# Hand-ordered ScalarE and VectorE queues in the mixers' main stretch, with softmax and weight parts staged a quarter chunk apart

## The chip, the cores and the metric

The kernel runs on one core of one Trainium2 chip. The metric is the device time of one execution in microseconds (us), the median of several executions.

## The reference

A two-layer encoder over 256 tokens with 1024 channels, everything in fp32. Each layer adds half a SwiGLU block, then three parallel token mixers, then half a second SwiGLU block:

```
x = x + 0.5 * swiglu(rmsnorm(x), w_ffn1_in, w_ffn1_out)
h = rmsnorm(x)
qa, ka, va, qb, kb, vb, qc, kc, vc, gate_logits = split(h @ w_in)
y_a = softmax attention, 8 heads on 2 key heads, q/k rmsnorm and axial rotary
y_b = windowed attention, 8 heads on 2 key heads, bias, a sink logit in the sum
y_c = 4 heads of (softmax1 - lambda * softmax2), bias, rmsnorm of the output
x = x + sum_n(sigmoid(gate_n) * (y_n @ w_branch_n)) @ w_out
x = x + 0.5 * swiglu(rmsnorm(x), w_ffn2_in, w_ffn2_out)
```

After the second layer a last rmsnorm gives the output.

## The kernel before

**Products in three parts.** Every fp32 operand of a big product is split in a high part (rounded to fp32r) and a low part (the rest), and `mm3` (L318) issues three matmuls for each product: high by high, high by low, low by high. The weights come in chunks of 1 MB. For each chunk SP issues a load into a `raw` tile (three buffers), ScalarE casts it to `hi` in two halves (L306) and VectorE subtracts to get `lo` (L307), each with three buffers. `weights()` (L312) hands out chunk i; before that it issues loads up to chunk i+4 and the splits up to chunk i+2, both halves one after the other.

**The mixer's main stretch.** `mixer(l)` first projects keys, queries and values of mixer A and turns the keys into `kas` (L999 to L1002, under `high_priority`). Then it walks a generator `rest()` (L925) over the other chunks in the order of `ORDER` (L39): queries of B, gates (g), keys and queries of C, and the branch products (r). A chunk `fm` (L814) is 48 matmuls on TensorE and yields four times, 0.5 credits each, so a yield is a quarter of a chunk, and a chunk counts 2.0. Its result leaves PSUM on VectorE; for a gate a Tanh on ScalarE follows at once (L847).

**The steps.** 24 softmax units (8 heads of A, 8 of B, 4 of C with two maps each) run through a plan of 32 steps. In step s, TensorE transposes the probabilities of unit s-3 (`transpose_p`, L611), makes the value product of unit s-5 (`pv`, L628), and makes the scores of unit s (`scores`, L604). For a unit of A or B these are four 128-column transposes, four matmuls and four matmuls. Round the scores lie a maximum on VectorE, two Exp on ScalarE, a reciprocal on VectorE and two scalings on ScalarE (`normalize`, L648). Round the transposes lie `pth` (ScalarE, L617) and `ptl` (VectorE, L618). Behind the value product lies `head_out` (L636): a copy on ScalarE (L638) and an add on VectorE (L639). `half()` (L101) gives the value product one of two halves of a single PSUM bank in turn. The loop at L1012 takes a step for every 1.25 credits (`PACE`), and the first as soon as 1.25 are there; it starts with 0.75, and the first yield adds 0.5. The first step is therefore issued behind the first quarter of chunk b1. The steps also issue SP's loads of the bias tiles `G` (L623). C's queries and keys are split in pieces that the list `later` hands out one by one.

**What sets the order.** TensorE follows the program. ScalarE and VectorE follow the program only inside `manual_schedule(engines=BY_HAND)`, which here stands round the start and round the last product of the kernel; everywhere else, the mixers included, a scheduler orders their instructions when the program is compiled. SP and POOL are always ordered by it.

Of the kernel before, what the change touches and what calls it, by code (L numbers as in the profile page):

```python
# [31 lines left out]
NBK = 32  # L32


PACE = 1.25
D1, D2, D3 = 3, 2, 2


# [29 lines left out]
def encoder(ctx: ExitStack, tc: tile.TileContext, a, rope, onehot, out):  # L68
# [240 lines left out]

    used = [0]  # L310

    def weights(more=True):  # L312
        i = used[0]
        used[0] += 1
        ahead(i + 5, i + 3 if more else i + 2)
        return parts[i]

    def mm3(ps, w, k, sl, xh, xl, first, last, start=None):  # L318
# [334 lines left out]
    def mixer(l):  # L653
        T = {}

        def soft_a(h):
            sc = scores(T["qa"][h // 4], (h // 2) % 2, h % 2, T["kas"], h // 4)
            sA = T["sA"]
            nb = sm.tile([P, 2], F32, name="nb")
            nc.vector.reduce_max(out=nb, in_=sc, axis=AX.X)  # L660
            nc.vector.scalar_tensor_tensor(out=nb, in0=nb, scalar=-1.0, in1=sA[:, :, h], op0=ALU.mult, op1=ALU.mult)
            e = t2("e")
            su = sm.tile([P, 2], F32, name="su")
            for qt in range(2):
                nc.scalar.activation(out=e[:, qt, :], in_=sc[:, qt, :], func=AF.Exp, bias=nb[:, qt:qt + 1], scale=sA[:, qt, h:h + 1], accum_out=su[:, qt:qt + 1])
            normalize(e, su)
            return e

        def biased(sc, G, init, su):

            nb = sm.tile([P, 2], F32, name="nb")
            e = t2("e")
            for qt in range(2):
                u0 = 128 * (1 - qt)
                nc.vector.tensor_tensor_reduce(out=e[:, qt, :], in0=sc[:, qt, :], in1=G[:, u0:u0 + S], scale=1.0, scalar=init, op0=ALU.add, op1=ALU.min, accum_out=nb[:, qt:qt + 1])
            for qt in range(2):
                nc.scalar.activation(out=e[:, qt, :], in_=e[:, qt, :], func=AF.Exp, bias=nb[:, qt:qt + 1], scale=-1.0, accum_out=su[:, qt:qt + 1])
            return e, nb

        def soft_b(h):  # L680
            sc = scores(T["qb"][h // 4], (h // 2) % 2, h % 2, T["kbs"], h // 4)
            sk = sink[:, l, h:h + 1]
            su = sm.tile([P, 2], F32, name="su")
            e, nb = biased(sc, T["G", h], nsink[:, l, h:h + 1], su)
            es = sm.tile([P, 2], F32, name="es")
            nc.scalar.activation(out=es, in_=nb, func=AF.Exp, bias=sk)
            nc.vector.tensor_add(su, su, es)
            normalize(e, su)
            return e

        def soft_c(h, mp):
            if mp == 0:
                T["suc"] = sm.tile([P, 2, 2], F32, name="suc")
            su = T["suc"]
            sc = scores(T["qc"][h // 2], h % 2, mp, T["kcs"][h // 2], mp)
            e, _ = biased(sc, T["G", B_HEADS + h], 3.0e38, su[:, mp, :])
            if mp == 0:
                T["e0"] = e
                return None

            e0 = T["e0"]
            ra, es = sm.tile([P, 2], F32, name="ra"), sm.tile([P, 2], F32, name="es")
            nc.vector.reciprocal(out=ra, in_=su[:, 1, :])
            nc.vector.scalar_tensor_tensor(out=ra, in0=ra, scalar=nlam[:, l:l + 1], in1=su[:, 0, :], op0=ALU.mult, op1=ALU.mult)
            for qt in range(2):
                nc.vector.scalar_tensor_tensor(out=e0[:, qt, :], in0=e[:, qt, :], scalar=ra[:, qt:qt + 1], in1=e0[:, qt, :], op0=ALU.mult, op1=ALU.add)
            nc.vector.scalar_tensor_tensor(out=es, in0=su[:, 0, :], scalar=EPS, in1=su[:, 0, :], op0=ALU.mult, op1=ALU.mult)
            return e0, es

        def out_c(h, pt, es):  # L710
            ph, pl = pt
            o = bank(acc, "oc")
            for qt in range(2):
                for kt in range(2):
                    rhs = T["vc"][:, kt, h // 2].rearrange("p a d -> p (a d)")
                    nc.tensor.matmul(o[:, qt, :], lhsT=ph[:, kt, cs(qt)], rhs=rhs, start=(kt == 0), stop=False)
                    nc.tensor.matmul(o[:, qt, :], lhsT=pl[:, kt, cs(qt)], rhs=rhs, start=False, stop=(kt == 1))
            of = t1("of").rearrange("p (a b) -> p a b", a=2)
            nc.vector.reduce_sum(out=of, in_=o.rearrange("p q (t d) -> p q d t", t=2), axis=AX.X)
            rc = sm.tile([P, 2], F32, name="rc")  # L720
            sq = t1("sqc")
            for qt in range(2):
                nc.scalar.activation(out=sq[:, :P], in_=of[:, qt, :], func=AF.Square, accum_out=rc[:, qt:qt + 1])
            nc.vector.scalar_tensor_tensor(out=rc, in0=rc, scalar=1.0 / P, in1=es, op0=ALU.mult, op1=ALU.add)
            nc.gpsimd.tensor_tensor(out=rc, in0=rc, in1=mhalf[:, 0:2], op=ALU.pow)
            for qt in range(2):
                nc.scalar.activation(out=of[:, qt, :], in_=of[:, qt, :], func=AF.Identity, scale=rc[:, qt:qt + 1])
            return of

        def turn_c(h, of):  # L730
# [5 lines left out]
            nc.scalar.activation(out=yh[:, h, :], in_=yt, func=AF.Identity, scale=g)  # L736
            nc.vector.scalar_tensor_tensor(out=yl[:, h, :], in0=yt, scalar=g, in1=f(yh[:, h, :]), op0=ALU.mult, op1=ALU.subtract)


        NU = 24  # L740
        plan = [[] for _ in range(NU + D1 + D2 + D3 + 1)]

        def ab_unit(u):
            br, h = u // 8, u % 8
            pair, par = h // 2, h % 2

            def s1():
                if h == 0:
                    T["y", br] = ytiles("ab"[br])
                T["e", u] = (soft_a if br == 0 else soft_b)(h)  # L750

            def s2():
                T["pt", u] = transpose_p(T.pop(("e", u)))

            def s3():
                if par == 0:
                    T["yp"] = t1("y")
                o = pv(T.pop(("pt", u)), T["vab"], 2 * br + pair // 2)
                with tc.high_priority():
                    head_out(o, par, T["yp"])  # L760
                if par == 1:
                    pair_out(T["yp"], pair, *T["y", br])

            plan[u + D1 + D2].append((1, s3))
            plan[u + D1].append((0, s2))
            plan[u].append((3, s1))

        def c_unit(h):
            u = 16 + 2 * h

            def s1(mp):
                if h == 0 and mp == 0:
                    T["yc"] = ytiles("c")
                T["e", u] = soft_c(h, mp)

            def s2():
                e, T["es", u] = T.pop(("e", u))
                T["pt", u] = transpose_p(e)

            def s3():  # L780
                T["of", h] = out_c(h, T.pop(("pt", u)), T.pop(("es", u)))

            def s4():
                turn_c(h, T.pop(("of", h)))

            plan[u + D1 + D2 + D3 + 1].append((2, s4))
            plan[u + D1 + D2 + 1].append((1, s3))
            plan[u + D1 + 1].append((0, s2))
            plan[u].append((3, lambda: s1(0)))
            plan[u + 1].append((3, lambda: s1(1)))  # L790
# [21 lines left out]


        def fm(evac):  # L814
            w = weights()
            ps = bank(wk, "fm")
            for i in range(4):
                project(ps, w, i // 2, range(i % 2 * KT // 2, (i % 2 + 1) * KT // 2))
                if i == 3:
                    evac(ps)  # L820
                yield 0.5

        def queries(key):
            def evac(ps):
                q = t2(key)
                nc.vector.scalar_tensor_tensor(out=q, in0=ps, scalar=-0.125, in1=bc(state["R"], 2), op0=ALU.mult, op1=ALU.mult)
                T.setdefault(key, []).append(split_q(q, key, later if key == "qc" else None))
            return evac

        def keys_c(ps):  # L830
# [6 lines left out]
        def gate(i, c):  # L837
# [6 lines left out]
            def evac(ps):  # L844

                nc.vector.tensor_mul(g, ps, bc(state["R"], 2))
                nc.scalar.activation(out=g, in_=g, func=AF.Tanh, scale=0.5)  # L847

            return fm(evac)

# [22 lines left out]
        def branch(i, y, steps):  # L873
# [1 line left out]
            while done[0] < steps:  # L875
                step()
            for n in range(2):
                w = weights()
                ps = [bank(wk, "br") for _ in range(2)]
                if n == 0:  # L880
                    products(ps[0], w, y, 0, (0, 1))
# [19 lines left out]
        def branch_c(y, steps):  # L901
# [5 lines left out]
                products(ps[mp], w, y, mp, range(3))  # L907
            while done[0] < len(plan):
                step()
            w1 = weights(False)  # L910
            ps1 = [bank(wk, "br")]
            products(ps1[0], w1, y, 0, range(3))
# [96 lines left out]
            for v, src in parts_v:  # L1009
                nc.vector.scalar_tensor_tensor(out=v[:, tt, :, 1, :], in0=src, scalar=r[:, tt:tt + 1], in1=f(v[:, tt, :, 0, :]), op0=ALU.mult, op1=ALU.subtract)  # L1010

        credit = PACE - 0.5  # L1012
        for n, more in enumerate(others):
            credit += more
            if n % 2 and later:
                later.pop(0)()
            while done[0] < len(plan) and credit >= PACE:
                credit -= PACE
                step()

        accs = [bank(acc, "wacc") for _ in range(4)]

# [108 lines left out]
```

## Time and profile before

| | |
|---|---|
| median of 3 runs | 1197.86 us (1197.07 to 1198.01) |
| the profiled execution | 1198.35 us |
| its span, first to last instruction | 1196.5 us |
| mean granted TensorE clock | 0.992 |
| TensorE busy | 1173.8 us, 98% of the span |
| VectorE busy | 849.0 us, 71% |
| ScalarE busy | 671.8 us, 56% |
| GpSimd busy | 246.8 us, 21% |
| read from memory | 215.59 MB, 184 GB/s over the span |

The busy times are sums over the span; a matmul counts as busy from its issue to its end, so matmuls that overlap hide short waits. The first mixer's main stretch lies between about 229 and 394 us of the span, the second's between about 818 and 982 us.

### The profile page before, as it was taken

How to read it: one execution, taken by the hardware profiler on the slowest of the kernel's cores; microseconds unless marked ns; L12 is line 12 of the kernel's file. 1: busy time of each engine (PE TensorE's matmuls, PEld its weight loads, DVE VectorE, ACT ScalarE, POOL GpSimd, SP SyncE). 2: the span in 40 equal slices, each digit the busy share in tenths (PEclk: the TensorE clock that was granted, in tenths of full speed). 3: DMA queues.
4: the chain of work that ended last, by engine and by line, in shares of the span. 5: the costliest groups of instructions: out<-in, count | busy, mean ns of one | idle time of the engine just before them, and what ended most of it. 6: DMA issues, size and time to landing. Idle time of an engine off the chain costs nothing.

```text
span 1196.5 us, 23210 instructions
## 1 busy us (share of the span) xinstructions
PE 1173.8 (98%) x9752; PEld 1151.8 (96%) x9752; DVE 849.0 (71%) x1155; ACT 671.8 (56%) x1130; POOL 246.8 (21%) x184
## 2 busy tenths in 40 slices
PE   9999999899999999999999999998999999999997
PEld 9999999799999999999999999998999999999996
DVE  7766568878896776666676666696789868656664
ACT  6444447589965554434454343466998556543443
POOL 1222124200011132212232222241000202221221
PEclk9999999899999999999999999998999999999999
DMA  8668565444455565656555565544455446555550
GB/s 284 232 203 307 192 205 177 141 142 145 163 162 177 175 207 181 202 186 211 177 177 201 186 211 179 193 159 141 142 173 166 141 170 199 198 190 180 198 186 36
DMA packets 170212, 218.15 MB, mean 182 GB/s; under 512 B 4382, under 2 KB 148304, under 8 KB 170108
## 3 DMA queue, kind: packets, MB, share of 16 engines
q1 hardware_dynamic: 169100, 215.09, 54.3%
q8 instruction: 76, 1.25, 0.4%
q10 hardware_dynamic: 864, 1.06, 0.3%
q0 software_dynamic: 144, 0.52, 0.1%
q14 instruction: 28, 0.23, 0.1%
HBM read 215.59 MB, written 4.22 MB: 184 GB/s over the span
## 4 chain that ended last, share of the span: by engine, by line
PE 81%; ACT 7%; DVE 6%; issue 3%; POOL 1%; DMA 1%; POOLq 0%; SPq 0%; ACTq 0%; DVEq 0%
PE gu L324 13%; PE gu L323 13%; PE gu L325 13%; PE facc L325 5%; PE facc L323 5%; PE facc L324 5%; PE fm L324 4%; PE fm L323 4%; PE fm L325 4%; ACT hi L306 2%; DVE lo L307 2%; PE facc L410 2%; PE facc L409 2%; PE br L323 2%; PE br L325 2%
## 5 line engine op out<-in xcount | busy, mean ns | idle before, releaser
L307 DVE TENSOR_TENSOR lo<-raw,hi 128x1024 fp32r<-128x1024 f32 (+1 forms) x396 | 539.3, 1374 | 143.8 <-ACT hi L306 142.9
L306 ACT CAST hi<-raw 128x1024 fp32r<-128x1024 f32 (+1 forms) x396 | 404.9, 1038 | 404.5 <-issue 358.4
L323 PE MATMUL gu<-xgh,hi 128*128 128x256 f32 x1408 | 390.7, 277 | 0.0
L324 PE MATMUL gu<-xgl,hi 128*128 128x256 f32 x1408 | 390.0, 277 | 0.3 <-DVE xgl L338 0.3
L325 PE MATMUL gu<-xgh,lo 128*128 128x256 f32 x1408 | 389.0, 276 | 0.0
L324 PEld LDWEIGHTS gu<-xgl,hi 128*128 128x128 f32 x1408 | 264.6, 188 | 1.9 <-DVE xgl L338 0.7
L323 PEld LDWEIGHTS gu<-xgh,hi 128*128 128x128 f32 x1408 | 264.3, 188 | 1.3 <-ACT hi L306 0.9
L325 PEld LDWEIGHTS gu<-xgh,lo 128*128 128x128 f32 x1408 | 264.3, 188 | 0.0
L323 PE MATMUL fm<-xgh,hi 128*128 128x256 f32 x640 | 181.8, 284 | 0.0
L324 PE MATMUL fm<-xgl,hi 128*128 128x256 f32 x640 | 180.8, 283 | 0.0
L325 PE MATMUL fm<-xgh,lo 128*128 128x256 f32 x640 | 180.2, 282 | 0.0
L487 POOL TENSOR_TENSOR gr<-gr,R 128x512 f32<-128x512 f32 x44 | 78.1, 1776 | 360.3 <-ACT gr L486 360.3
L324 PEld LDWEIGHTS fm<-xgl,hi 128*128 128x128 f32 x640 | 122.4, 191 | 0.7
L325 PEld LDWEIGHTS fm<-xgh,lo 128*128 128x128 f32 x640 | 123.0, 192 | 0.0
L323 PEld LDWEIGHTS fm<-xgh,hi 128*128 128x128 f32 x640 | 122.4, 191 | 0.1
L323 PE MATMUL facc<-hh,hi 128*128 128x256 f32 x384 | 106.0, 276 | 0.0
L325 PE MATMUL facc<-hh,lo 128*128 128x256 f32 x384 | 106.0, 276 | 0.0
L324 PE MATMUL facc<-hl,hi 128*128 128x256 f32 x384 | 106.0, 276 | 0.0
L499 POOL TENSOR_TENSOR hl<-hid,hh 128x512 fp32r<-128x512 f32 x35 | 61.7, 1763 | 124.4 <-ACT hh L498 124.4
L485 DVE TENSOR_TENSOR gr<-gu,R 128x512 f32<-128x512 f32 x44 | 30.4, 690 | 73.8 <-PE gu L325 73.7
L323 PEld LDWEIGHTS facc<-hh,hi 128*128 128x128 f32 x384 | 72.1, 188 | 0.0
L325 PEld LDWEIGHTS facc<-hh,lo 128*128 128x128 f32 x384 | 72.1, 188 | 0.0
(234 smaller groups left out, 1926.1 us busy)
## 6 DMA issues: line engine op xcount, KB each, us to landing
raw<-in_w_ffn_in_dram SPq DMA_DIRECT2D x86, 1024.0 KB, 5.1
raw<-in_w_ffn_out_dram SPq DMA_DIRECT2D x44, 1024.0 KB, 5.0
raw<-in_w_in_dram SPq DMA_DIRECT2D x38, 1024.0 KB, 5.1
raw<-in_w_branch_dram SPq DMA_DIRECT2D x12, 1024.0 KB, 5.1
raw<-in_w_out_dram SPq DMA_DIRECT2D x8, 1024.0 KB, 4.9
G<-skew SPq DMA_DIRECT2D x24, 192.0 KB, 4.2
raw<-in_w_in_dram SPq DMA_DIRECT2D x8, 512.0 KB, 5.4
skew<-vec_d SPq DMA_DIRECT2D x6, 512.0 KB, 7.9
```

What stands on the lines that cost most here:

```text
L306: nc.scalar.copy(out=hi[:, h], in_=raw[:, h])
L307: nc.vector.tensor_sub(lo[:, h], raw[:, h], f(hi[:, h]))
L323: nc.tensor.matmul(ps, lhsT=hi[:, k, sl], rhs=xh, start=st, stop=False, **chk)
L324: nc.tensor.matmul(ps, lhsT=hi[:, k, sl], rhs=xl, start=False, stop=False, **chk)
L325: nc.tensor.matmul(ps, lhsT=lo[:, k, sl], rhs=xh, start=False, stop=last, **chk)
L409: nc.tensor.matmul(ps, lhsT=xh[:, k, cs(tt)], rhs=w[1][:, k, sl], start=False, stop=False)
L410: nc.tensor.matmul(ps, lhsT=xl[:, k, cs(tt)], rhs=w[0][:, k, sl], start=False, stop=(last and k == 1))
L485: state["gr"] = nc.vector.tensor_mul(gr, ps, Rb)
L487: nc.gpsimd.tensor_mul(gr, gr, Rb)
L499: nc.gpsimd.tensor_sub(hl, hid, f(hh))
```

## The change

`manual_schedule(engines=BY_HAND)` is put round the loop of the main stretch. The softmax functions become generators: `run` executes one up to its first `yield`, and `onward`, called at every quarter chunk, carries each one stage on. The gates' Tanh comes one quarter later (`soon`), B's queries are split in pieces like C's, and `weights(slow=True)` leaves the split of chunk i+2 to two half splits that the loop issues in the first and third quarter of the current chunk. Credits start at -2.0 with a first price of 0, so that the first step is issued behind the fourth quarter of b1; later prices are 1.15, 1.4 and 1.1 credits for steps done below 8, below 16 and from 16 on.

```diff
...
-PACE = 1.25
+LEAD = 2.0
+PACES = [1.15, 1.4, 1.1]
 D1, D2, D3 = 3, 2, 2
...
-    def weights(more=True):
+    pending = []
+    def weights(more=True, slow=False):
         i = used[0]
         used[0] += 1
-        ahead(i + 5, i + 3 if more else i + 2)
+        while pending:
+            pending.pop(0)()
+        ahead(i + 5, i + 3 if more and not slow else i + 2)
+        if slow and len(parts) == i + 2 and i + 2 < len(specs):
+            g = split(2)
+            pending.extend([lambda: next(g), lambda: next(g)])
         return parts[i]
     def mm3(ps, w, k, sl, xh, xl, first, last, start=None):
...
             nc.vector.scalar_tensor_tensor(out=nb, in0=nb, scalar=-1.0, in1=sA[:, :, h], op0=ALU.mult, op1=ALU.mult)
+            yield
             e = t2("e")
...
                 nc.scalar.activation(out=e[:, qt, :], in_=sc[:, qt, :], func=AF.Exp, bias=nb[:, qt:qt + 1], scale=sA[:, qt, h:h + 1], accum_out=su[:, qt:qt + 1])
+            yield
             normalize(e, su)
...
                 nc.vector.tensor_tensor_reduce(out=e[:, qt, :], in0=sc[:, qt, :], in1=G[:, u0:u0 + S], scale=1.0, scalar=init, op0=ALU.add, op1=ALU.min, accum_out=nb[:, qt:qt + 1])
+            yield
             for qt in range(2):
...
             su = sm.tile([P, 2], F32, name="su")
-            e, nb = biased(sc, T["G", h], nsink[:, l, h:h + 1], su)
+            e, nb = yield from biased(sc, T["G", h], nsink[:, l, h:h + 1], su)
             es = sm.tile([P, 2], F32, name="es")
             nc.scalar.activation(out=es, in_=nb, func=AF.Exp, bias=sk)
+            yield
             nc.vector.tensor_add(su, su, es)
...
             sc = scores(T["qc"][h // 2], h % 2, mp, T["kcs"][h // 2], mp)
-            e, _ = biased(sc, T["G", B_HEADS + h], 3.0e38, su[:, mp, :])
+            e, _ = yield from biased(sc, T["G", B_HEADS + h], 3.0e38, su[:, mp, :])
             if mp == 0:
...
+            yield
             e0 = T["e0"]
...
                 nc.scalar.activation(out=sq[:, :P], in_=of[:, qt, :], func=AF.Square, accum_out=rc[:, qt:qt + 1])
+            yield
             nc.vector.scalar_tensor_tensor(out=rc, in0=rc, scalar=1.0 / P, in1=es, op0=ALU.mult, op1=ALU.add)
             nc.gpsimd.tensor_tensor(out=rc, in0=rc, in1=mhalf[:, 0:2], op=ALU.pow)
+            yield
             for qt in range(2):
...
+        running = []
+        def run(g, key=None):
+            def go():
+                r = yield from g
+                if key:
+                    T[key] = r
+            running.append(go())
+            next(running[-1])
+        def onward(n=1):
+            for _ in range(n):
+                for g in list(running):
+                    if next(g, running) is running:
+                        running.remove(g)
+        def soon(f):
+            def g():
+                yield
+                f()
+            run(g())
...
             def s1():
...
                     T["y", br] = ytiles("ab"[br])
-                T["e", u] = (soft_a if br == 0 else soft_b)(h)
+                run((soft_a if br == 0 else soft_b)(h), ("e", u))
             def s2():
...
             def s1(mp):
...
                     T["yc"] = ytiles("c")
-                T["e", u] = soft_c(h, mp)
+                run(soft_c(h, mp), ("e", u))
             def s2():
...
             def s3():
-                T["of", h] = out_c(h, T.pop(("pt", u)), T.pop(("es", u)))
+                run(out_c(h, T.pop(("pt", u)), T.pop(("es", u))), ("of", h))
             def s4():
...
         def fm(evac):
-            w = weights()
+            w = weights(slow=True)
             ps = bank(wk, "fm")
...
             def evac(ps):
...
                 nc.vector.scalar_tensor_tensor(out=q, in0=ps, scalar=-0.125, in1=bc(state["R"], 2), op0=ALU.mult, op1=ALU.mult)
-                T.setdefault(key, []).append(split_q(q, key, later if key == "qc" else None))
+                T.setdefault(key, []).append(split_q(q, key, later))
             return evac
         def keys_c(ps):
             def evac(ps):
                 nc.vector.tensor_mul(g, ps, bc(state["R"], 2))
-                nc.scalar.activation(out=g, in_=g, func=AF.Tanh, scale=0.5)
+                soon(lambda: nc.scalar.activation(out=g, in_=g, func=AF.Tanh, scale=0.5))
...
             for n in range(2):
-                w = weights()
+                w = weights(slow=True)
                 ps = [bank(wk, "br") for _ in range(2)]
...
                 step()
+                onward(3)
             w1 = weights(False)
...
-        credit = PACE - 0.5
+        credit, pace = -LEAD, 0.0
+        stack = tc.manual_schedule(engines=BY_HAND)
+        stack.__enter__()
         for n, more in enumerate(others):
             credit += more
+            onward()
             if n % 2 and later:
                 later.pop(0)()
-            while done[0] < len(plan) and credit >= PACE:
-                credit -= PACE
+            while done[0] < len(plan) and credit >= pace:
+                credit -= pace
                 step()
+                pace = PACES[min(done[0] // 8, 2)]
+            if pending and n % 2 == 0:
+                pending.pop(0)()
+        stack.__exit__(None, None, None)
...

```

## Rows read from the trace of the kernel before

**Rows 1.** The page, part 1 (busy time) and part 4 (chain by engine).

```profile
PE 1173.8 (98%) x9752; PEld 1151.8 (96%) x9752; DVE 849.0 (71%) x1155; ACT 671.8 (56%) x1130; POOL 246.8 (21%) x184
...
PE 81%; ACT 7%; DVE 6%; issue 3%; POOL 1%; DMA 1%; POOLq 0%; SPq 0%; ACTq 0%; DVEq 0%
```

**Rows 2.** Waits of TensorE, whole span: us in total, times, longest us.

```profile
PE sc L608 <- ACT kas L579: 8.0, 2, 4.0
PE halves L632 <- DVE y L639: 4.0, 4, 1.7
```

**Rows 3.** Windows round both first steps: stretch, length, busy per engine, granted clock, DMA.

```profile
230.60:232.80 2.20, 0.02 (x1) 0.00 (x0) 2.20 (x5) 0.96 (x2) 0.00 (x0) 1.00 1.07 377
...
234.60:239.60 5.00, 4.74 (x20) 4.45 (x21) 4.83 (x10) 2.43 (x4) 0.00 (x0) 0.50 0.34 117
...
823.40:828.50 5.10, 4.76 (x20) 4.47 (x21) 4.93 (x10) 2.48 (x5) 0.00 (x0) 0.50 0.35 120
828.50:830.00 1.50, 1.50 (x9) 1.50 (x8) 0.12 (x1) 1.29 (x2) 0.00 (x0) 0.50 0.65 158
```

**Rows 4.** Timeline of VectorE ahead of the first step: start, us, what.

```profile
229.42 2.35 DVE L307 TENSOR_TENSOR lo<-raw,hi 128x1024 fp32r<-128x1024 f32 x2
...
232.47 0.68 DVE L826 SCALAR_TENSOR_TENSOR qb<-fm,R 128x512 f32<-128x512 f32 x1
233.07 0.41 DVE L1001 TENSOR_TENSOR ka<-kqg,ps_e 128x256 f32<-128x256 f32 x1
233.40 1.22 DVE L307 TENSOR_TENSOR lo<-raw,hi 128x1024 fp32r<-128x1024 f32 x1
...
235.84 0.42 DVE L581 TENSOR_TENSOR kas<-ka,kas 64x256 fp32r<-64x256 f32 x1
```

**Rows 5.** Groups of TensorE instructions, whole span: busy us, mean ns, idle before.

```profile
L632 PE MATMUL halves<-pth,vab 128*128 128x256 f32 x64 | 19.2, 322 | 4.1 <-DVE y L639 4.0
...
L633 PE MATMUL halves<-ptl,vab 128*128 128x256 f32 x64 | 16.5, 280 | 0.0
...
L608 PE MATMUL sc<-kas,qa 128*128 128x256 f32 x64 | 12.4, 313 | 8.5 <-ACT kas L579 8.0 <-DVE kas L581 0.5
...
L608 PE MATMUL sc<-kbs,qb 128*128 128x256 f32 x64 | 10.1, 280 | 0.0
```

**Rows 6.** Timeline of TensorE round one step and one quarter chunk.

```profile
253.56 0.60 PE L615 MATMUL pt<-ident,e 128*128 128x128 f32 x4
...
254.47 0.29 PE L323 MATMUL fm<-xgh,hi 128*128 128x256 f32 x1
...
255.17 0.28 PE L323 MATMUL fm<-xgh,hi 128*128 128x256 f32 x1
...
256.53 0.28 PE L323 MATMUL fm<-xgh,hi 128*128 128x256 f32 x1
```

**Rows 7.** The page, part 6: loads of w_in, KB each, us to landing.

```profile
raw<-in_w_in_dram SPq DMA_DIRECT2D x38, 1024.0 KB, 5.1
```

**Rows 8.** Timeline of three engines round one wait for head_out.

```profile
288.56 0.39 PE L632 MATMUL halves<-pth,vab 128*128 128x256 f32 x1
...
293.06 0.37 ACT L638 COPY y<-halves 64x256 f32<-64x256 f32 x1
...
294.27 0.41 DVE L639 TENSOR_TENSOR y<-y,halves 64x256 f32<-64x256 f32 x1
...
294.74 0.38 PE L632 MATMUL halves<-pth,vab 128*128 128x256 f32 x1 [1.71 <-DVE y L639]
```

**Rows 9.** Windows from b1 to the 16th unit, both layers: PE, PEld, DVE, ACT, POOL busy.

```profile
229.00:311.00 82.00, 76.06 (x630) 74.92 (x628) 67.10 (x137) 71.68 (x163) 4.11 (x5) 0.96 0.48 156
818.00:900.00 82.00, 76.85 (x632) 76.12 (x632) 67.28 (x139) 73.07 (x165) 5.34 (x6) 0.96 0.49 162
```

**Rows 10.** Waits in 229 to 394 us, all engines: us in total, times, longest.

```profile
ACT e L665 <- DVE nb L661: 3.9, 3, 2.7
...
ACT e L651 <- DVE su L649: 1.8, 3, 0.7
```

## The prediction

> **What bounds the kernel now.** I began with the page's busy times and its chain. TensorE is busy 1173.8 us of a 1196.5 us span, and 81% of the chain runs over it [rows 1]. So time is to be had only where TensorE waits or is slow. The list of TensorE's waits names two places, both in the mixers' main stretch [rows 2]. The first scores of mixer A wait for the split keys `kas`, once in each layer, 4.0 us each. The value products wait for `head_out` of the head before, 4.0 us in four longer waits.
>
> The windows show a second price of the first place [rows 3]. The granted clock is still at 1.00 (2.4 GHz) in the first 2.2 us of the wait, and at 0.50 (1.2 GHz) for 5.0 us of work behind it in layer 0 and for 6.6 us in layer 1. Work at half speed loses half its time: 2.5 + 3.3 = 5.8 us, of which some 0.3 us fall on waiting inside these windows. I take 5.5.
>
> Why `kas` is late stands in VectorE's timeline [rows 4]. The engine is busy without a gap; a weight split of 2.35 us, the evacuation `qb` and other work stand before `ka`, and one more half split of 1.22 us before its last parts, which are ready at 235.84 + 0.42 = 236.26. The program issues the first step behind only one quarter of b1.
>
> The second place also hides waits under the overlap of matmuls. The first matmul of a value product takes 322 ns on average, its partner 280 [rows 5]: 64 x 42 ns = 2.7 us beside the 4.0 us idle. The timeline of one wait shows the course [rows 8]. A value product runs at 288.56, but ScalarE copies its result only at 293.06 and VectorE adds it at 294.27; the next product starts at 294.74. The copy stood late in ScalarE's queue, not late for want of data.
>
> **The first step, three quarters later.** Twelve matmuls of a quarter take 256.53 - 255.17 = 1.36 us [rows 6]; a credit is two quarters, 2.72 us, a chunk 5.44. TensorE therefore comes to the first scores 3 x 1.36 = 4.08 us later with work done, against a first wait of 4.0 and a second of 0.25 per layer (8.0 and 0.5 in all, [rows 5]). With `kas` at the same time, TensorE, idle from 230.6 [rows 3] before, would come at about 234.7, find the first parts, and wait some 0.7 us for the rest. As the wait before lay 2.2 us at full clock, one of 0.7 should leave the clock alone. Gain: 8.5 + 5.5 - 1.4 = 12.6 us. Bounds: 14.0 if the rest fits too, 2.4 in the rival below.
>
> The split of chunk g00 leaves the place ahead of `ka` and comes with b1, so VectorE has up to 2.35 us less in front of the keys; but TensorE needs it right behind the first scores. The work due by then is all that [rows 4] show up to 236.26 less the half split of g01 (1.22), thus 235.0, and TensorE is at g00 at 234.7 plus its scores (0.45). It just fits; the 0.7 us stand for either.
>
> **Pace of the steps.** First step at 2.0 credits, the 8th at 2.0 + 7 x 1.15 = 10.05, the 16th at 10.05 + 8 x 1.4 = 21.25, the 32nd at 21.25 + 16 x 1.1 = 38.85, before the last branch at 40. Before, the 16th was at 19.25 and the 32nd at 39.25. The products of branch 0 and 1 at 24 and 28 need 13 and 21 steps and find 18 and 22. So no step is forced, and the end costs nothing.
>
> **Half splits in two quarters, Tanh and B's queries later.** The instructions are the same and no chunk loses its cover: the split of chunk i+2 is due two chunks after chunk i starts, 10.9 us, and is issued by its third quarter. A weight load takes 5.1 us [rows 7] and gets its buffer within chunk i-1; only the load behind g00's split starts some 3 us later than now, and still lands before its own split needs it within about 1 us. That is a wait of ScalarE, not of TensorE. The steps' bias loads on SP shift with the steps and keep their lead of two steps. POOL has 4.11 us of work in 82 [rows 9], so what it gets later costs nothing. All this: 0, with a bound of 1 us per layer against it.
>
> **Program order for ScalarE and VectorE.** The copy and add of `head_out` now stand right behind the split of the same step's transposes. A value product then waits only if ScalarE runs late by more than a step: 1.15 x 2.72 plus a step's own 0.91 [rows 6] and 0.45 for the value product is 4.5 us, at 1.4 credits 5.2; less copy and add (0.37 and 0.41, [rows 8]) and their hand-overs it leaves about 4.0. I take the 4.0 us idle as gone and half of the hidden 2.7: 5.3 us. Bounds: 6.7, and 0.
>
> Against it stands head-of-line waiting on ScalarE. From b1 to the 16th unit it had 71.68 us of work in layer 0 and 73.07 in layer 1, each in 82 us [rows 9]. With TensorE's waits gone, TensorE needs 21.25 x 2.72 = 57.8 us plus the steps (3 x 0.45 + 2 x 0.91 + 11 x 1.36 = 18.1), 75.9 us, to the same point. ScalarE may be 4.0 us later: 79.9. Its room for idling is 8.2 and 6.8 us, 15.0 together; before, it idled 10.3 and 8.9, 19.2 together. If program order leaves that idling as it is, TensorE waits 4.2 us anew; if the quarter between stages removes the waits for VectorE ahead of Exp and scaling (3.9 and 1.8 us in layer 0, [rows 10]), 0. I take 3.0, nearer to the idling that rows show.
>
> One rule speaks against this part. The Trainium skill, PSUM — Partial Sum Buffer, section Engine vs sequencer instructions, says that the queues of ScalarE, VectorE and GpSimdE are strictly first in, first out. By it an instruction that waits holds up all behind it, under either ordering, and a written order can be worse than a planned one; the sum would then be the slower rival's. The trace agrees with the first half: the copy at 293.06 was held 4 us by its place in the queue [rows 8].
>
> **Sum.** -12.6 - 5.3 + 3.0 = -14.9 us. The profiled execution took 1198.35, so 1183.45; the median of the runs shown lies 0.49 lower: 1183.0.
>
> **Rivals.**
> - *All waits go.* 14.0 + 6.7 = 20.7 us: 1177.2. For it: both waits come from places in queues, not from missing work. Against it: ScalarE's room is smaller than its present idling. Chance 0.12.
> - *The wait moves to the keys or to g00.* The part before the loop is still ordered by the scheduler. If g00's split lands ahead of `ka` once more, or its low half stays behind other work, TensorE waits 0.7 + 2.35 = 3.05 us per layer, beyond the 2.2 us that the clock stood before, and 5.5 us of clock come back. The first term shrinks to 14.0 - 6.1 - 5.5 = 2.4 us: 1193.2. For it: VectorE has no gap there [rows 4]. This also covers that program order does not reach the instructions that make the first step late. Chance 0.18.
> - *Slower: scaling waits behind the half split.* In program order a unit's reciprocal stands behind the low half split on VectorE (1.22 us, [rows 4]), and ScalarE's next instruction is the scaling that needs it. If ScalarE so idles 1.3 us at each of 32 units, 41.6 us exceed its room of 15.0 by 26.6 us: 1183.0 - 3.0 + 26.6 = 1206.6. It decides from (15.0 + 17.9) / 32 = 1.03 us per unit, where the gains without new waits (12.6 + 5.3) are used up; today it idles 19.2 / 32 = 0.6. Against it: the scaling comes a quarter behind the Exp. Chance 0.07.
>
> **How the numbers follow.** The forecast, about 1179 to 1189 by its bounds, has a chance of 0.60. With the three rivals that makes 0.97; 0.03 is left for no change to speak of. The range from 1177.0 to 1192.0 holds the forecast, the first rival and near half of the second, and leaves out the rest. A measurement of this kernel can tell 0.2%, 2.4 us, from no change. Faster than that: 0.60 + 0.12 + 0.17 = 0.89; within it: 0.04; slower: 0.07.
>
> **What would show it.** Right: TensorE's waits name `kas` with under 1 us per layer, no window of the mixers has a clock of 0.50, `head_out`'s copy starts within 2 us of its product, and the first matmul of a value product is near 280 ns. ScalarE's busy time from b1 to the 16th unit stays at 72 to 73 us while the stretch shrinks to about 78. Wrong: a clock of 0.50 behind the first scores or behind g00's first matmul (second rival); a wait of scalings for the reciprocal above 1 us each, with value products or transposes waiting in step (third); or TensorE's waits in chunks for `hi` or `lo`, which would break the cover I gave the half splits.

## The result, and the profile after

The changed kernel takes 1296.99 us (median of 4 runs, 1296.87 to 1297.43) against 1197.67 before: a ratio of 1.0829, interval 1.0816 to 1.0842. It is 99 us slower, and the forecast of 1183.0 fell with its range and its sign. All of it lies in the two mixers: the last product of the first mixer starts at 442.5 us of the span where it started at 394.5, that of the second at 1081.5 where it started at 982.4. The page's lines that answer to [rows 1]:

```profile
PE 1205.1 (93%) x9752; PEld 1176.6 (91%) x9752; DVE 854.9 (66%) x1155; ACT 675.3 (52%) x1130; POOL 246.4 (19%) x184
...
PE 65%; DVE 16%; ACT 12%; issue 5%; POOL 2%; POOLq 0%; ACTq 0%; DVEq 0%
```

The work of VectorE, ScalarE and GpSimd is what it was within 1%. What changed is the chain: VectorE and ScalarE held 6% and 7% of it and now hold 16% and 12%. TensorE's waits (us in total, times, longest us) answer to [rows 2]:

```profile
PE halves L641 <- DVE y L648: 55.3, 20, 7.3
PE halves L749 <- ACT of L743: 10.8, 4, 4.6
PE br L332 <- DVE tmp L904: 6.8, 2, 3.4
PE sc L617 <- ACT e L675: 3.0, 2, 1.5
PE pt L624 <- DVE ptl L627: 2.5, 2, 1.2
PE sc L617 <- DVE kas L590: 1.2, 2, 0.6
```

The wait for `kas` fell from 8.5 us to 1.2, as forecast. The wait of the value products for `head_out`, which should have gone, grew from 4.0 us to 55.3. Windows of the first mixer show what that does to the clock (stretch, length, busy of PE, PEld, DVE, ACT, POOL, clock, DMA):

```profile
231.00:235.00 4.00, 3.92 (x35) 3.72 (x33) 4.00 (x6) 1.98 (x5) 0.00 (x0) 1.00 0.87 285
235.00:241.00 6.00, 5.46 (x47) 5.46 (x48) 5.27 (x10) 2.94 (x5) 0.00 (x0) 1.00 0.61 194
264.00:270.50 6.50, 0.02 (x1) 0.00 (x0) 2.22 (x5) 4.25 (x10) 0.00 (x0) 0.67 0.24 76
270.50:277.00 6.50, 5.65 (x28) 5.65 (x29) 2.85 (x6) 3.53 (x9) 0.00 (x0) 0.54 0.25 86
```

Round the first scores, at 234.6, the clock now stays at 1.00, where [rows 3] had 0.50. Thirty us later TensorE stands still for a whole window, and the work behind it runs near half clock. The mean clock of the run is 0.968, against 0.992.

The two engines behind it, from b1 to the 16th unit (the stretch of [rows 9], which took 82 us):

```profile
229.00:347.20 118.20, 89.53 (x676) 86.61 (x675) 72.09 (x144) 75.44 (x168) 3.61 (x5) 0.89 0.37 117
866.00:985.60 119.60, 89.29 (x675) 86.17 (x674) 71.97 (x144) 76.56 (x169) 4.28 (x6) 0.89 0.38 120
```

ScalarE has about 76 us of work in 119 and VectorE 72; neither is full. They wait for each other. In the first of these stretches (engine, what it waits for, us in total, times, longest us):

```profile
ACT e L660 <- DVE su L658: 17.5, 13, 2.2
ACT e L675 <- DVE nb L670: 9.0, 6, 3.0
ACT gates L886 <- DVE gates L885: 4.7, 4, 1.9
...
DVE lo L308 <- ACT hi L307: 23.8, 14, 2.4
DVE ptl L627 <- ACT pth L626: 12.3, 9, 2.0
```

One round of it, in the timeline of both engines (start, us, what, and in brackets the idle time before and its releaser):

```profile
316.78 1.03 ACT L307 CAST hi<-raw 128x1024 fp32r<-128x1024 f32 x1
317.84 1.22 DVE L308 TENSOR_TENSOR lo<-raw,hi 128x1024 fp32r<-128x1024 f32 x1 [1.97 <-ACT hi L307]
318.98 0.68 DVE L885 TENSOR_TENSOR gates<-fm,R 128x512 f32<-128x512 f32 x1
319.70 0.63 ACT L886 ACTIVATE gates<-gates 128x512 f32<-128x512 f32 x1 [1.89 <-DVE gates L885]
320.24 0.57 ACT L626 CAST pth<-pt 128x512 fp32r<-128x512 f32 x1
320.84 0.69 DVE L627 TENSOR_TENSOR ptl<-pt,pth 128x512 fp32r<-128x512 f32 x1 [1.17 <-ACT pth L626]
...
322.29 0.51 ACT L689 ACTIVATE e<-e,nb 128x256 f32<-128x256 f32 x1 [1.09 <-DVE nb L686]
...
323.47 1.03 ACT L307 CAST hi<-raw 128x1024 fp32r<-128x1024 f32 x1
324.54 1.23 DVE L308 TENSOR_TENSOR lo<-raw,hi 128x1024 fp32r<-128x1024 f32 x1 [1.88 <-ACT hi L307]
...
325.87 0.17 DVE L658 RECIPROCAL su<-su 128x2 f32<-128x2 f32 x1
326.13 0.91 ACT L660 ACTIVATE e<-e,su 128x256 f32<-128x256 f32 x2 [1.62 <-DVE su L658]
```

Read it as a relay. VectorE waits until `hi` is done, then makes `lo`; ScalarE stands meanwhile, since its next instruction needs what VectorE does behind `lo`: the gate's product, or the reciprocal. Then VectorE waits for `pth`, ScalarE for the maximum, and so round again. For much of the round one of the two works and the other waits: of these 118.2 us ScalarE idles 42.8 and VectorE 46.1, and the three lines for ScalarE above hold 31.2 of its 42.8.

### The profile page after: what moved, and what is told of

It reads as the page before. It is cut to its first block, busy times and chain, and to the rows that moved or that the text cites. A ratio compares the mean times of both kernels' runs of the same rounds, so it can differ in the third digit from the quotient of the medians.

```text
span 1295.2 us, 23199 instructions
## 1 busy us (share of the span) xinstructions
PE 1205.1 (93%) x9752; PEld 1176.6 (91%) x9752; DVE 854.9 (66%) x1155; ACT 675.3 (52%) x1130; POOL 246.4 (19%) x184
## 4 chain that ended last, share of the span: by engine, by line
PE 65%; DVE 16%; ACT 12%; issue 5%; POOL 2%; POOLq 0%; ACTq 0%; DVEq 0%
PE gu L333 12%; PE gu L332 12%; PE gu L334 12%; DVE lo L308 6%; PE facc L334 5%; PE facc L332 5%; PE facc L333 5%; ACT hi L307 4%; ACT e L660 2%; DVE ptl L627 2%; PE facc L419 2%; PE facc L418 1%; PE facc L417 1%; ACT e L689 1%; PE fm L333 1%
## 5 line engine op out<-in xcount | busy, mean ns | idle before, releaser
L332 PE MATMUL fm<-xgh,hi 128*128 128x256 f32 x640 | 188.1, 294 | 0.0
L333 PE MATMUL fm<-xgl,hi 128*128 128x256 f32 x640 | 186.8, 292 | 0.0
L334 PE MATMUL fm<-xgh,lo 128*128 128x256 f32 x640 | 185.8, 290 | 0.0
L332 PEld LDWEIGHTS fm<-xgh,hi 128*128 128x128 f32 x640 | 129.6, 203 | 0.1
L333 PEld LDWEIGHTS fm<-xgl,hi 128*128 128x128 f32 x640 | 128.9, 201 | 0.7
L334 PEld LDWEIGHTS fm<-xgh,lo 128*128 128x128 f32 x640 | 129.1, 202 | 0.0
L641 PE MATMUL halves<-pth,vab 128*128 128x256 f32 x64 | 22.7, 372 | 55.3 <-DVE y L648 55.3
L333 PEld LDWEIGHTS facc<-hl,hi 128*128 128x128 f32 x384 | 72.1, 188 | 0.0
```

Source lines behind the costliest of these rows:

```text
L332: nc.tensor.matmul(ps, lhsT=hi[:, k, sl], rhs=xh, start=st, stop=False, **chk)
L333: nc.tensor.matmul(ps, lhsT=hi[:, k, sl], rhs=xl, start=False, stop=False, **chk)
L334: nc.tensor.matmul(ps, lhsT=lo[:, k, sl], rhs=xh, start=False, stop=last, **chk)
L641: nc.tensor.matmul(o, lhsT=v[:, kt, vi], rhs=h[:, kt, :], start=(kt == 0), stop=False)
```

## The experiments

All ratios are against the kernel before, run on the same chip. Theory A: with both queues in program order each engine waits for the other at nearly every instruction. Theory B: stages, half splits or paces cost the time, not the order. Theory C: one engine's program order is enough.

### Which part of the change costs the time

**Order taken away.**

```diff
-        stack = tc.manual_schedule(engines=BY_HAND)
-        stack.__enter__()
...
-        stack.__exit__(None, None, None)
```

> The changed kernel without the written order of ScalarE and VectorE in the main stretch: stages, half splits, late first step and paces stay. If the loss is the written order itself (the two engines wait for each other in turn, theory A): faster than before, 1180 to 1192 us, first-step wait and low clock gone, waits for head_out 2 to 8 us in all. If the loss is the stages, half splits or paces (theory B): above 1270 us, with the long waits for head_out still there.

Measured: 1204.51 us, ratio 1.0058 (1.0041 to 1.0075). Neither range holds it, but 92 of the 99 us are gone with this one edit: B is out. The rest is still slower than before, with 9.6 us of waits for `head_out`.

**Order alone.** The kernel before with the same three lines round its loop.

> The kernel before with only the written order round the loop: whole softmax units and whole splits, no stages, first step early. Theory A: at least as slow as the changed kernel, 1290 to 1380 us, because without stages each Exp, reciprocal and scaling follow at once and the two engines alternate more tightly. Theory B: near before, 1190 to 1210 us.

Measured: 1288.15 us, 1.0754 (1.0732 to 1.0775), within 2 us of A's range and far from B's. The written order needs no stage to lose; the stages don't save it. Which wait carries the loss depends on what is written: here, from 229 to 365 us, ScalarE waits mostly for the maximum and little for the reciprocal.

```profile
ACT e L665 <- DVE nb L661: 14.8, 7, 2.7
...
ACT e L651 <- DVE su L649: 5.8, 16, 0.5
```

**Whole splits.**

```diff
-            w = weights(slow=True)
+            w = weights()
```

> The changed kernel with whole splits at the start of a chunk in place of half splits in two quarters. If the half splits' place is what makes the engines alternate (low half ahead of the reciprocal, my third rival as I put it): most of the loss goes, below 1240 us. If any tight order of the two engines does it (theory A): 1275 to 1330 us.

Measured: 1276.79 us, 1.0659 (1.0638 to 1.0680): A's range. Half splits make it worse by 20 us, not better. That they hand the relay over at two places of a chunk may be the reason; no run shows it.

**One engine's order at a time.**

```diff
-        stack = tc.manual_schedule(engines=BY_HAND)
+        stack = tc.manual_schedule(engines={mybir.EngineType.Activation})
```

> The changed kernel with the written order for ScalarE alone in the main stretch; VectorE is planned again. If the loss needs both queues fixed, so that each waits for the other (theory A): most of it goes, 1200 to 1230 us, and VectorE's waits for ScalarE's casts fall under a third. If a late ScalarE queue alone is enough (theory C, ScalarE bound by its own order): above 1260 us.

> The changed kernel with the written order for VectorE alone; ScalarE is planned again. Theory A: 1200 to 1230 us. Theory C: as far as ScalarE's own order is the culprit, 1200 to 1215 us, near the version with both planned; if VectorE's order is it, above 1260 us.

Measured: ScalarE alone 1217.69 us, 1.0163 (1.0143 to 1.0184); VectorE alone 1204.50 us, 1.0053 (1.0033 to 1.0073). With both planned it was 1204.5. So VectorE's written order adds nothing, ScalarE's 13 us, and both together 92: the loss needs both, as A says, and C is out. With ScalarE alone written, VectorE's waits for ScalarE's casts `hi` and `pth` fall from 36.1 us (above) to 10.8. With VectorE alone written, the waits between the two in the stretch of the first 16 units are these:

```profile
ACT e L675 <- DVE nb L670: 2.6, 3, 1.6
...
DVE ptl L627 <- ACT pth L626: 6.4, 6, 2.1
...
DVE lo L308 <- ACT hi L307: 1.0, 2, 0.9
```

I read this as the planner fitting the free queue to the fixed one: VectorE's wait for `hi` falls from 23.8 us to 1.0.

### Where the relay closes

**Stages two quarters apart.** Each `yield` of a softmax stage becomes two.

> The changed kernel with its softmax stages two quarters apart in place of one, half splits as they are. If the mutual waits come from too little other work between a stage and the one it needs (theory A): a third or more of the loss goes, 1215 to 1265 us, and ScalarE's waits for the reciprocal and the maximum halve. If the distance means nothing once ScalarE is late: 1285 to 1310 us.

Measured: 1287.64 us, 1.0747 (1.0726 to 1.0769): only 9 us come back, so the second range holds and the share that I expected of theory A does not. From 229 to 365 us ScalarE's waits for the maximum of mixer A fell from 9.0 us to 2.0, but those for the reciprocal rose from 19.1 us to 33.3:

```profile
ACT e L660 <- DVE su L658: 33.3, 16, 3.1
...
ACT e L675 <- DVE nb L670: 2.0, 1, 2.0
```

One leg opened and another closed harder. I take it that once both queues are late, what counts is which instructions stand between two that depend on each other, not the time between them; this run alone does not prove it.

**Low half a quarter behind the high half.**

```diff
             nc.scalar.copy(out=hi[:, h], in_=raw[:, h])
+            if apart:
+                yield
             nc.vector.tensor_sub(lo[:, h], raw[:, h], f(hi[:, h]))
...
             onward()
+            if pending and n % 2 == 1:
+                pending.pop(0)()
```

> The changed kernel with the low half of a split a quarter chunk behind its high half, behind the next stage's reciprocal. If the reciprocal behind the low half is the edge that closes the circle (my third rival's place): ScalarE's wait for the reciprocal falls under 12 us of 38, 1215 to 1255 us. If any neighbouring pair closes it again (maximum, ptl): 1270 to 1300 us.

**Scaling on GpSimd, written order.** ScalarE neither scales nor waits for the reciprocal.

```diff
-        for qt in range(2):
-            nc.scalar.activation(out=e[:, qt, :], in_=e[:, qt, :], func=AF.Identity, scale=su[:, qt:qt + 1])
+        nc.gpsimd.tensor_tensor(out=e, in0=e, in1=su.unsqueeze(2).to_broadcast([P, 2, S]), op=ALU.mult)
```

> The changed kernel, written order, with the scaling on GpSimd: ScalarE neither does it nor waits for the reciprocal. If that leg of the circle carries the loss: 1200 to 1250 us. If the circle closes over exp and ptl instead: above 1265 us.

**Both.**

> Both edits together: low halves a quarter later and the scaling on GpSimd, in written order. If the written order loses only by these two legs: 1182 to 1215 us. If a written order of both engines loses whatever its detail: above 1230 us.

Measured: 1244.12 us, 1.0384 (1.0363 to 1.0404), for the low half later; 1256.82, 1.0490 (1.0470 to 1.0511), for GpSimd; 1226.36, 1.0232 (1.0215 to 1.0249), for both. A low half a quarter later gives back 53 us, more than half of the loss. ScalarE's wait for the reciprocal in the whole span, in the changed kernel and with the low half later:

```profile
ACT e L660 <- DVE su L658: 38.2, 28, 2.2
...
ACT e L662 <- DVE su L660: 14.3, 16, 1.2
```

The time lies in the first range, but the wait missed the 12 us that I had set for it. The edit also moves the low half away from its high half, and VectorE's waits for `hi` fell with it, from 26.3 us to 15.6 between 229 and 365 us, so this run does not part the two. The run with GpSimd takes the wait of the scaling alone out of ScalarE's queue, along with the scaling's own work, and gives back 40 us. Together they make the low half and the reciprocal behind it the largest leg of the changed kernel. The second and third run lie between their two ranges: waits for the maximum and `ptl` are left, and no version with both orders written came nearer than 2.3% to the kernel before.

### Why the late first step brought nothing either

**Late first step alone, planned order.**

```diff
-PACE = 1.25
+PACE = 1.2
...
-        credit = PACE - 0.5
+        credit = PACE - 2.0
```

> The kernel before with only the first step behind the fourth quarter of b1, and a pace of 1.2 so that the steps end where they did. If my first term was right: 12.6 us less, 1183 to 1188 us, no clock of 0.50 behind the first scores. If the wait moves to g00's weights (second rival): 1192 to 1196 us, with a low clock behind the scores or behind g00's first matmul.

Measured: 1197.49 us, 0.9998 (0.9989 to 1.0007): no change, which neither range holds. The window behind the first scores and TensorE's waits:

```profile
234.60:239.60 5.00, 4.55 (x38) 4.33 (x38) 4.87 (x10) 3.42 (x6) 0.00 (x0) 1.00 0.34 118
```

```profile
PE halves L632 <- DVE y L639: 12.0, 12, 1.6
PE sc L608 <- ACT e L665: 1.6, 1, 1.6
...
PE sc L608 <- DVE kas L581: 0.9, 2, 0.4
```

The step did what I forecast: 0.9 us of waiting for the keys and full clock, with 38 matmuls in the window that held 20. Behind it the waits for `head_out` grew from 4.0 to 12.0 us in twelve pieces, and the last product of the first mixer starts at 394.1 us, where it started at 394.5. The pace of 1.2 packs the steps of mixers A and B closer than before, which could by itself eat the gain; the next run takes that away.

**With the paces, then with ScalarE's load cut.** The second run adds the paces 1.15, 1.4 and 1.1; the third also puts the scaling on GpSimd as above.

> The kernel before with the late first step and the paces 1.15, 1.4, 1.1, planned order, no stages, whole splits. If the pace of 1.2 alone ate the gain of the late first step in the second run (it gave 18.0 credits from the 1st to the 16th step against 18.75 before and 19.25 here): 1187 to 1193 us. If ScalarE and VectorE bound mixers A and B whatever the pace: 1195 to 1200 us, 16th scores of layer 0 again near 310 us.

> The ninth version (late first step, paces, planned order) with the scaling of mixers A and B on GpSimd, one 128x512 product per unit, in place of two ScalarE instructions. If ScalarE's load bounds mixers A and B there (16 units x 0.91 us = 14.6 us per layer taken off it): the waits for head_out go and the late first step shows its gain, 1180 to 1188 us. If VectorE, the planned order or the shared work with GpSimd bounds: 1193 to 1205 us.

Measured: 1197.03 us, 0.9995 (0.9986 to 1.0005), and 1196.42, 0.9988 (0.9979 to 0.9997): the second range for both. So the pace was not what ate the gain. The run with GpSimd is 1.5 us faster than the kernel before, not the 10 us and more that I looked for. Less load on ScalarE is worth little here.

**Place of the splits, planned order.** Half splits added to each of these two versions, and to the one without GpSimd a rule that a split stands behind the last `head_out` in both queues:

```diff
+            with ExitStack() as behind:
+                for k in ("copy", "add"):
+                    if k in state:
+                        behind.enter_context(tc.issue_after(state[k].ins))
```

> The eighth version (late first step, paces, planned order, scaling on GpSimd) with half splits in the first and third quarter of a chunk. If VectorE's whole low halves ahead of head_out's add hold the value products (the timeline shows 3.2 us of them): waits for head_out fall from 7.1 to under 3 us, 1188 to 1193 us. If the total load of the two engines bounds mixers A and B: 1195 to 1199 us, 16th scores of layer 0 near 311 us.

> The ninth version (late first step, paces, planned order, scaling on ScalarE) with half splits in the first and third quarter. If the place of the whole splits is what takes the late step's gain back: 1187 to 1193 us, waits for head_out from 9.3 to under 4 us. If it is load: 1195 to 1200 us.

> The fourteenth version with each half split of the main stretch also queued behind the last head_out's copy on ScalarE and add on VectorE, all else planned. If only that one place in the two queues costs the waits: under 2 us for head_out, 1184 to 1190 us. If the written place brings back mutual waits: 1200 to 1230 us. If load bounds: 1194 to 1199 us.

Measured: 1198.07 us, 1.0002 (0.9994 to 1.0011); 1201.24, 1.0035 (1.0021 to 1.0048); 1201.77, 1.0036 (1.0023 to 1.0049). None gains. The first lies in the range for load, the second just above it, and the third at the foot of the range for mutual waits; but the third differs from the second by 0.5 us, within the noise, so the rule neither helps nor harms. Against the same version with whole splits (1197.03) the half splits cost 4.2 us. Neither place frees the value products.

**Less load, more time.** In the first run five gate chunks of each mixer use the parts of the chunk before, so five splits are left out and those gates are computed with the wrong weights; the other two have the paces 1.4, 1.45, 0.95, with the scaling on GpSimd and without.

```diff
+        if len(parts) in shared:
+            parts.append(parts[-1])
+            return
```

> The ninth version (late first step, paces, planned order) in which five of each mixer's chunks (four gate chunks and C's first but one neighbour, all in the first 24 credits) are not split but use the parts of the chunk before: it leaves out five of the twelve splits there, 2.1 us of ScalarE and 2.4 us of VectorE each, and computes those projections with the wrong weights; TensorE's work and all loads stay. If the total load of the two engines in mixers A and B takes the late step's gain back: waits for head_out under 3 us, 1180 to 1188 us. If the order in the queues does it: above 1192 us.

> The eighth version (planned order, late first step, scaling on GpSimd) with paces 1.4, 1.45, 0.95: mixers A and B get 21.4 credits from the 1st to the 16th step in place of 19.25, mixer C less. If load in A and B bounds: 1188 to 1194 us, waits for head_out under 4 us. If the queues' order does, or C then becomes late: 1195 to 1203 us.

> The ninth version (scaling on ScalarE) with the same wide paces. Load: 1187 to 1194 us. Order, or a late C: 1195 to 1203 us.

Measured: 1199.70 us, 1.0016 (1.0006 to 1.0025); 1197.12, 0.9990 (0.9981 to 0.9999); 1200.51, 1.0022 (1.0013 to 1.0031). The second range holds for all three. All five of the chunks left out are gates. The first run has clearly less for both engines to do, 834.3 us for VectorE and 654.7 for ScalarE in the whole span against 852.8 and 671.7 with all splits, as its window to the 16th unit shows too (compare 67.10 and 71.68 in [rows 9]). It still waits, and some of the first step's wait for `kas` is back:

```profile
229.00:311.00 82.00, 78.26 (x653) 77.39 (x653) 62.07 (x130) 66.37 (x157) 2.96 (x4) 0.98 0.52 169
```

```profile
PE halves L637 <- DVE y L644: 7.2, 11, 1.2
PE sc L613 <- ACT kas L584: 3.3, 2, 1.8
```

So load by itself does not bound mixers A and B either. What is left is the planner's order as a whole: it was made anew for each of these programs, and each time placed `head_out` so that value products wait for it, here 0.7 us each on average (7.2 us in 11 waits), above 1.0 (12.0 in 12). One such wait, in the run with the late first step alone:

```profile
273.60 0.36 PE L632 MATMUL halves<-pth,vab 128*128 128x256 f32 x1
...
277.94 0.36 ACT L638 COPY y<-halves 64x256 f32<-64x256 f32 x1
...
279.20 0.42 DVE L639 TENSOR_TENSOR y<-y,halves 64x256 f32<-64x256 f32 x1
...
279.68 0.39 PE L632 MATMUL halves<-pth,vab 128*128 128x256 f32 x1 [1.63 <-DVE y L639]
```

From 273.60 to the copy ScalarE works almost without a gap, on casts of C's keys, two Exp and a half split; VectorE then has a half split ahead of the add. Over the 32 value products of mixers A and B the copy starts 2.6 us behind the start of its product on average in the kernel before, 3.6 us in this run, and 6.0 us in the changed kernel. Why the planner places it so is not settled: the kernel already issues `head_out` under `high_priority`, so in these programs a priority is not enough. The next product writes the other half of the bank and still starts only 0.06 us behind the add of the head just before, here as in [rows 8], so the two halves give `head_out` no step more. Two things were not tried: a planned order with `head_out` alone fixed at the front of both queues, and a bank of its own for each of the two halves.

## Why the prediction was wrong, point by point

- **First step, three quarters later: right as far as it goes.** I gave 0.7 us of waiting per layer and full clock; the changed kernel shows 0.6 and 1.00, the version with that edit alone 0.45 and 1.00. But I booked the whole 12.6 us to the end. In the planned order most of them came back within the mixers, 8.0 us more of waits for `head_out` and 1.6 us ahead of later scores, and the time did not change; where the rest went is not located.
- **Pace, half splits, cover of the weights: half right.** No matmul waits for `hi` or `lo`, so the cover held. That the edits cost nothing was wrong: whole splits are 20 us faster in the written order, and 4.2 us in the planned one.
- **Program order: the step that failed.** I wrote that "the copy and add of `head_out` now stand right behind the split of the same step's transposes" and that ScalarE's room was 15.0 us against an idling of 19.2, and took 3.0 us as "nearer to the idling that rows show". Those rows show the idling of an order that was planned to avoid it. In the written order ScalarE idles 118.20 - 75.44 = 42.8 us and 119.60 - 76.56 = 43.0: 85.8 us, 2.68 per unit against 0.6. I treated each engine as a queue with a load; what bounds is the chain that alternates between two, as a written order of either engine alone costs 13 us or nothing. `head_out` does stand where I put it, behind the cast `pth`, but ScalarE reaches it 6.0 us behind the product on average, more than the 4.0 us of slack that I had left it.
- **The gain behind the first matmul was no wait.** I read the 42 ns by which the first matmul of a value product is longer than its partner as 2.7 us of hidden waits, and booked half. In the kernel before it takes 0.36 us also where the add before it ended 2.1 us earlier, so 1.35 of the 5.3 us had no ground, and "near 280 ns" was no sign to look for.

```profile
266.06 0.42 DVE L639 TENSOR_TENSOR y<-y,halves 64x256 f32<-64x256 f32 x1
...
268.59 0.36 PE L632 MATMUL halves<-pth,vab 128*128 128x256 f32 x1
```

- **The slower rival had the place and the size of its wait, but not the rest.** I priced 1.3 us at each of 32 units, 41.6 us; the scalings waited 38.2 us for the reciprocal, 1.4 us in each of 28 waits, so its sign came true. But I took this wait for all of ScalarE's idling. The waits for the maximum, the gate's product and the others came on top, and made 85.8 us. With them the rival's own sum gives 85.8 - 15.0 = 70.8 us of new waits and 1250.8 us. The 46 us beyond that are not broken down; in them go a slower clock (TensorE's busy time for the same 9752 matmuls rose by 31.3 us) and waits in mixer C and the branches (10.8 and 6.8 us), of which I had none. I gave it 0.07 because "the scaling comes a quarter behind the Exp"; the version with two quarters gave 9 us back.
- **The rule that I set beside it** (the Trainium skill, PSUM — Partial Sum Buffer, section Engine vs sequencer instructions: ScalarE's and VectorE's queues are strictly first in, first out) should have weighed more. The trace agrees with it: in the relay above ScalarE stood for 1.89 us ahead of the gate's Tanh at 319.70, while the cast `pth` behind it, at 320.24, had had its four transposes since 310.3. What it costs when both queues are written so, the 79 and 92 us between one order written and both show.

## What to carry to other kernels

Before an order is written by hand for two engines that feed each other, write both queues side by side and follow the dependences across: an instruction that waits should find what it needs several instructions back in the other queue, counted in that queue. A quarter chunk of TensorE's time gave 9 us back between the softmax stages and 53 us behind the high half, so the time alone does not tell what it is worth. And a wait that is removed pays only if the next wait on the same path is shown to have slack; one edit alone on the chip tells that for little.

## What was not expected of the hardware

GpSimd's product of 128x512 values took 1.04 us at 284.00, and 1.85 us where it started beside VectorE's low halves, which for their part took 3.19 us for two where [rows 4] have 2.35. The timeline of both engines in the version with the scaling on GpSimd and planned order, and the least, median and longest of the two low halves in ns:

```profile
284.00 1.04 POOL L651 TENSOR_TENSOR e<-e,su 128x512 f32<-128x512 f32 x1 [4.02 <-DVE su L650]
...
287.09 3.19 DVE L308 TENSOR_TENSOR lo<-raw,hi 128x1024 fp32r<-128x1024 f32 x2
...
287.34 1.85 POOL L651 TENSOR_TENSOR e<-e,su 128x512 f32<-128x512 f32 x1 [2.30 <-DVE su L650]
...
L308 DVE TENSOR_TENSOR lo<-raw,hi x2: 1205/1634/2064, 287.1 to 288.2; 128x1024 fp32r<-128x1024 f32 x2
```

The first low half ran its usual 1.21 us, the product beside it took 0.81 us longer, and the second low half, begun at 288.2 beside the product, took 2.06 us. This agrees with what the Trainium skill, SBUF — State Buffer, section Who interferes with whom, states: a VectorE operation with two SBUF inputs and a GpSimd operation that reads SBUF exclude each other. It was rare here: the median of the 32 GpSimd products is 1.04 us, and the low halves of the first main stretch took 57.6 us against 55.1 with the scaling on ScalarE. So it explains little of why work taken off ScalarE this way gave so little.
